# Both branch products in one loop, x added to w_out by identity products, and w_down's first weights loaded during w_up

## The chip, the cores and the metric

One core of a Trainium2 chip runs the whole kernel. Its engines are TensorE (PE, matrix products; PEld is its loading of weights), VectorE (DVE), ScalarE (ACT), GpSimd (POOL) and SyncE (SP, which issues most DMAs). The metric is the device time of one run in microseconds (us). Before the change three runs took 1689.25, 1694.08 and 1695.91 us; the median is 1694.08.

## The reference

One step of a decoder layer. The 1024 prompt positions and 8 samples of 4 positions together are T = 1056 columns; all data are float32. The part that the change touches:

```python
    mix = (jax.nn.sigmoid(gate_a) * (attn_out @ w_branch_attn)      # 256 -> 1024
           + jax.nn.sigmoid(gate_s) * (ssm_out @ w_branch_ssm))     # 512 -> 1024
    x = x + mix @ w_out                                             # 1024 -> 1024

    up = rmsnorm(x, norm2_g) @ w_up                                 # 1024 -> 2 * 2816
    a, val = up[..., :D_FF], up[..., D_FF:]
    a_ext = jnp.concatenate([conv_buf.astype(a.dtype), a], axis=1)
    a_conv = conv_b
    for i in range(CONV_W):
        a_conv = a_conv + conv_w[i] * a_ext[:, i:i + s]
    conv_state = a_ext[:, s:]
    x = x + (jax.nn.silu(a_conv) * val) @ w_down                    # 2816 -> 1024
```

Ahead of it stand a norm, the combined projection `w_in`, dilated attention over prompt and cache, and a state-space branch that ends in a gated unit (GLU); behind it stands a last norm.

## The kernel before

**Layout.** An activation is held transposed: channels on the 128 partitions, the 1056 columns side by side, so 1024 channels are eight tiles (KD = 8). The columns are ordered in four residues of C = 264 (256 prompt positions and 8 sample ones each). A float32 product is made of three products of halves: every operand is split into a rounded part (`hi`, a cast on ACT) and the rest (`lo`, a subtraction on DVE), and PE adds lo·hi, hi·lo and hi·hi. `load_w` (lines 148 to 159) does that for weights: a DMA by SP into `wraw`, the cast into `whi` (L157), the subtraction into `wlo` (L158). `gemm_k` (L165 to L178) makes the products of one 128-row output tile in three PSUM banks of 352 columns each (CH = 352, NCH = 3).

**Order.** Up to line 1218 PE's order is written by hand. After it a scheduler orders each engine's queue by its own estimates; a tile that takes the place of a former one (a pool of few buffers, or a pool that is closed and opened again at the same address) brings waits with it. SP, ACT and POOL issue DMAs in the order of their queues, and a DMA that waits holds all that stand behind it in its queue.

**Stages around the change.** (1) The attention of the samples over the cache: `cache(g, b, 1)` loads value rows by POOL's queue into a pool of four buffers, 24 loads, and PE multiplies them into one PSUM tile `pD` (L1227, L1230); then a few short steps (L1233 to L1244) put the result into `attnF`. (2) The SSM branch (L1269 to L1279): for each of eight output tiles, 36 products of w_branch_ssm, the gate loaded from `sgd` in DRAM, sigmoid on ACT, three gate multiplications on DVE, and the tile written to `msd` in DRAM. (3) x is loaded again, transposed on PE (L1281 to L1299) and written to `xtd` in DRAM. (4) The attention branch (L1324 to L1337): 18 products per output tile, gate loads from `sgd`, loads from `msd`, sigmoid, multiplication on DVE, addition on POOL, split into `mh` and `ml`. (5) w_out (L1366 to L1387): per output tile 72 products; DVE adds the tile loaded from `xtd` and writes `y`, which also goes to DRAM (`yd2`). (6) w_up (`up(f)`, 22 times), with the operands in a form in which seven block products stand for eight; the hidden tile `gt` goes to DRAM (`hd`) by POOL's queue. (7) At the end of w_up 22 transposes of conv state, then w_down (L1561 to L1602): `hidden(q)` loads hidden tiles from `hd` and splits them, and `load_w` brings weight groups of four (24 products each) into a pool `w2` whose memory is free only when w_up's tiles are.

Of the kernel before, what the change touches and what calls it, by code (L numbers as in the profile page):

```python
# [9 lines left out]
F32 = mybir.dt.float32  # L10
# [89 lines left out]
def body(tc, I, O):  # L100
# [12 lines left out]
    with root:  # L113
# [1133 lines left out]
        msd = dr.tile([D, T], F32, name="msd")  # L1247
        s5_ = root.enter_context(ExitStack())
        gl = pool("gl", 1, stack=s5_)
# [31 lines left out]
        xraw, xcol = ([t[:, j] for t in x_pairs(n, F32) for j in range(2)] for n in ("xh", "xl"))  # L1281
        xsr = go.tile([P, T], F32, name="go")[:32, :D]
        nc.sync.dma_start(xsr, I['x_sample'].rearrange("b t d -> (b t) d"))
        for s in range(S4):
            for h in range(2):
                nc.sync.dma_start(xraw[2 * s + h][:, :D], xpv[h][:, s])
        pt = pa.tile([P, 512], F32, name="pa")
        for k in range(KD):
            tr(pt[:, k * 32:(k + 1) * 32], xsr[:, k * P:(k + 1) * P])
        for k in range(KD):  # L1290
            V_.tensor_copy(sc(xcol[k])[:, :, 256:], pt[:, k * 32:(k + 1) * 32].rearrange("p (b s) -> p s b", s=S4))
        for s in range(S4):
            for k2 in range(0, KD, 2):
                pt = pa.tile([P, 512], F32, name="pa")
                for k in range(2):
                    for h in range(2):
# [340 lines left out]
```

## Time and profile before

| what | value |
|---|---|
| median of three runs | 1694.08 us |
| profiled run, its own time | 1695.59 us |
| span of the profiled run | 1693.8 us |
| PE busy | 1576.6 us, 93% |
| DVE busy | 1020.9 us, 60% |
| granted TensorE clock, mean | 0.967 |

The profile is one execution. Its span runs from the first to the last instruction, and 1.8 us of that run's time lie outside. PE is the busiest engine, but its share is a mean: the stages named above are read one by one, by tables over windows of time. A busy PE at a granted clock of 0.5 does half the work. In rows of products a `pg<-yh,wlo` names the output tile and the two operands, buffer numbers left out.

### The profile page before, as it was taken

What the parts mean: (1) busy time and instruction counts of PE and PEld (TensorE: products, weight loads), DVE (VectorE), ACT (ScalarE), POOL (GpSimd) and SP (SyncE); (2) the same over time, 40 slices, a digit from 0 to 9 for tenths busy, and PEclk for the clock granted to TensorE, in tenths of its full rate; (3) what the DMA queues carried; (4) which work ended last, traced back from release to release, by engine and by line L of the source; (5) the groups of instructions that cost most, each with busy time, mean ns of one, the idle gap of its engine ahead of it and who ended that gap; (6) DMA issues with size and microseconds to landing.
All of it is one profiled execution on the core that took longest, in us unless ns stands there. A gap on an engine that the chain in (4) does not pass through costs nothing. (4 is left out here: it accounts for less than half of the span.)

```text
span 1693.8 us, 28884 instructions
## 1 busy us (share of the span) xinstructions
PE 1576.6 (93%) x11523; PEld 1501.7 (89%) x11523; DVE 1020.9 (60%) x1655; ACT 625.1 (37%) x1135; POOL 462.7 (27%) x479
## 2 busy tenths in 40 slices
PE   5999888999999988997799999999999986999997
PEld 5899877998888878876699999999999986999997
DVE  6545989233343534322755988888888874566453
ACT  5211221144344432323544433333333334555444
POOL 0669364012122322310612022222222220121211
PEclk9899989999999999998899999999999997999998
DMA  8263322355336444676833222222222238788662
GB/s 229 64 174 112 106 60 64 99 136 134 97 100 155 132 114 167 219 232 227 260 127 115 63 76 83 82 76 77 88 78 76 76 92 284 246 264 261 196 200 96
DMA packets 272656, 234.50 MB, mean 138 GB/s; under 512 B 33269, under 2 KB 252895, under 8 KB 272522
## 3 DMA queue, kind: packets, MB, share of 16 engines
q1 hardware_dynamic: 255458, 198.65, 38.9%
q0 software_dynamic: 6496, 23.43, 3.8%
q10 hardware_dynamic: 10568, 10.58, 1.9%
q8 instruction: 90, 1.47, 0.4%
q14 instruction: 44, 0.36, 0.1%
HBM read 184.12 MB, written 50.46 MB: 138 GB/s over the span
## 5 line engine op out<-in xcount | busy, mean ns | idle before, releaser
L158 DVE TENSOR_TENSOR wlo<-wraw,whi 128x1024 fp32r<-128x1024 f32 (+1 forms) x148 | 185.4, 1255 | 155.8 <-ACT whi L157 154.6
L176 PE MATMUL pg<-xh,wlo 128*128 128x352 f32 x816 | 215.0, 345 | 1.8 <-ACT pt__5401 L872 0.5
L176 PE MATMUL pg<-xh,whi 128*128 128x352 f32 x816 | 199.9, 326 | 0.0
L176 PE MATMUL pg<-xl,whi 128*128 128x352 f32 x816 | 199.6, 326 | 0.0
L157 ACT CAST whi<-wraw 128x1024 fp32r<-128x1024 f32 (+1 forms) x148 | 147.7, 1002 | 137.8 <-PE pd L1577 89.2
L176 PEld LDWEIGHTS pg<-xh,wlo 128*128 128x128 f32 x816 | 143.7, 192 | 13.2 <-issue 5.6
L176 PEld LDWEIGHTS pg<-xl,whi 128*128 128x128 f32 x816 | 145.1, 192 | 0.3
L176 PEld LDWEIGHTS pg<-xh,whi 128*128 128x128 f32 x816 | 144.9, 190 | 0.0
L964 POOL TENSOR_TENSOR qb<-kt,qb 128x512 f32<-128x512 f32 x48 | 65.9, 1385 | 245.4 <-DMA qb<-qd 163.0
L1581 POOL COPY sy<-y 128x8 f32<-128x8 f32 x32 | 31.5, 983 | 226.0 <-DVE y L1580 225.4
L187 ACT CAST sh<-S 128x512 fp32r<-128x512 f32 x88 | 52.2, 619 | 77.1 <-DVE S L1452 52.0
L1484 POOL TENSOR_TENSOR cv<-cv,rb 128x1056 f32<-128x1056 f32 x22 | 54.2, 2464 | 72.9 <-ACT cv L1483 72.9
L1009 ACT COPY pTs<-pT 128x256 f32<-128x256 f32 (+1 forms) x48 | 22.6, 470 | 124.0 <-PE pT L145 122.1
L188 DVE TENSOR_TENSOR sl<-S,sh 128x512 fp32r<-128x512 f32 x88 | 60.6, 693 | 0.0
L176 PE MATMUL pg<-yh,wlo 128*128 128x352 f32 x144 | 48.8, 350 | 7.6 <-ACT go L473 4.9
L1480 ACT ACTIVATE cv<-ext,cw 128x1056 f32<-128x1056 f32 x22 | 28.0, 1271 | 72.8 <-POOL ext L1476 72.6
L176 PE MATMUL pg<-mh,wlo 128*128 128x352 f32 x192 | 47.5, 329 | 6.1 <-DVE wlo L158 6.1
L1467 DVE TENSOR_TENSOR ext<-ext,rb 128x528 f32<-128x528 f32 x22 | 48.5, 2207 | 0.7
L176 PE MATMUL pg<-ml,whi 128*128 128x352 f32 x192 | 47.3, 328 | 0.0
L176 PE MATMUL pg<-mh,whi 128*128 128x352 f32 x192 | 46.8, 325 | 0.0
L176 PE MATMUL pg<-yl,whi 128*128 128x352 f32 x144 | 46.5, 333 | 0.0
L176 PE MATMUL pg<-yh,whi 128*128 128x352 f32 x144 | 46.4, 335 | 0.0
(1046 smaller groups left out, 4941.2 us busy)
## 6 DMA issues: line engine op xcount, KB each, us to landing
wraw<-in_w_down_dram SPq DMA_DIRECT2D x80, 512.0 KB
wraw<-in_w_up_dram SPq DMA_DIRECT2D x44, 512.0 KB
wraw<-in_w_in_dram SPq DMA_DIRECT2D x38, 512.0 KB
qb<-qd SPq DMA_DIRECT2D x48, 256.0 KB
hd<-gt POOLq DMA_DIRECT2D x22, 528.0 KB, 3.0
wraw<-hd SPq DMA_DIRECT2D x44, 264.0 KB
sgd<-go SPq DMA_DIRECT2D x16, 528.0 KB
kt<-in_cache_kv_w_dram SPq DMA_DIRECT2D x32, 256.0 KB
```

The source lines that it names most:

```text
L157: A_.copy(hi, raw)
L158: E2.tensor_tensor(lo, raw, hi.bitcast(F32), OP.subtract)
L176: PE.matmul(ps[c][:, :CH], wt[:, k0 + k, m0:m0 + P], xt[:, c * CH:(c + 1) * CH], start=k == 0 and j == 0, stop=k == n - 1 and j == 2)
L187: A_.copy(hi, src)
L188: V_.tensor_tensor(lo, src, hi.bitcast(F32), OP.subtract)
L964: G_.tensor_tensor(qb, kv_, qb, OP.mult)
L1009: A_.copy(pTs[:, :2 * n * P], pT[:, :2 * n * P])
L1467: V_.tensor_tensor(e[:, 2:4], e[:, 2:4], h2(rb2[:, H1]), OP.mult)
L1480: A_.activation(cv, ef[:, 0:T], AF.Identity, bias=cw[:, 3, f:f + 1], scale=cw[:, 0, f:f + 1])
L1484: G_.tensor_tensor(cv, cv, rb2, OP.mult)
L1581: G_.tensor_copy(sy[:, m + x].rearrange("p (b s) -> p b s", s=S4)[:, :, q], y[:, m + x, 256:])
```

## The change

Three edits. First, SSM and attention branch become one loop: per output tile both gates are loaded, both products made, multiplied, added on POOL and split; nothing goes through `msd`. The loop uses eight PSUM banks, which are opened only when the PSUM tiles of stage (1) are closed; weights of both branches and of w_out share the pool `wo` of two buffers. Second, x is not transposed and stored ahead. `x_rows` loads rows of x as they lie in DRAM into tiles that later hold w_up's operands, and `add_x` multiplies them by a 128-column identity inside the PSUM accumulation of w_out; DVE then only copies PSUM out. The identity products are plain float32, not split. Third, the last two hidden tiles are split straight from `gt`, the first hidden loads and two weight groups of w_down are issued while w_up ends, through the pool of w_up's weights.

The core of the diff (left out are changes of names and the place of a few pools):

```diff
-        for m in range(KD):
-            if m % 2 == 0:
-                w = load_w(I['w_branch_ssm'][0][:, m * P:(m + 2) * P], 4, mw=2 * P)
-            ps = gbanks()
-            gemm(ps, w, list(zip(sh, sl)), m0=m % 2 * P)
-            t = go.tile([P, T], F32, name="go")
-            nc.sync.dma_start(t, sgd[1, m * P:(m + 1) * P])
-            A_.activation(t, t, AF.Sigmoid)
-            for c in range(NCH):
-                V_.tensor_tensor(t[:, cs(c)], ps[c][:, :CH], t[:, cs(c)], OP.mult)
-            nc.scalar.dma_start(msd[m * P:(m + 1) * P], t)
...
-            for k2 in range(0, KD, 2):
-                pt = pa.tile([P, 512], F32, name="pa")
-                for k in range(2):
-                    for h in range(2):
-                        tr(pt[:, (2 * k + h) * P:(2 * k + h + 1) * P], xraw[2 * s + h][:, (k2 + k) * P:(k2 + k + 1) * P])
-                for k in range(2):
-                    A_.copy(xcol[k2 + k][:, s * C:s * C + 256], pt[:, 256 * k:256 * k + 256])
-        xtd = dr.tile([D, T], F32, name="xtd")
-        for k in range(KD):
-            nc.sync.dma_start(xtd[k * P:(k + 1) * P], xcol[k])
...
         psum(8)
         rbp = pool("rbp", 1)
         wb = pool("wo", 2)
-        ck = pool("ck", 12, stack=s6a, side="right")
+        s6 = root.enter_context(ExitStack())
+        mp = pool("mp", 1, stack=s6)
+        mh = [mp.tile([P, T], F32R, name=f"mh{k}") for k in range(KD)]
+        ml = [mp.tile([P, T], F32R, name=f"ml{k}") for k in range(KD)]
+        ck = pool("ck", 4, stack=gst, side="right")
+        wa = None
         for m in range(KD):
+            if m % 2 == 0:
+                w = load_w(I['w_branch_ssm'][0][:, m * P:(m + 2) * P], 4, mw=2 * P, pw=wb)
             if m % 4 == 0:
-                w = load_w(I['w_branch_attn'][0][:, m * P:(m + 4) * P], 2, mw=4 * P, pw=wb)
-            ps = gbanks()
-            gemm(ps, w, list(zip(ah, al)), m0=m % 4 * P)
-            for c in range(NCH):
-                t = ck.tile([P, CH], F32, name="ck")
-                nc.sync.dma_start(t, sgd[0, m * P:(m + 1) * P, cs(c)])
+                wa = load_w(I['w_branch_attn'][0][:, m * P:(m + 4) * P], 2, mw=4 * P, pw=wb)
+            gs, ga = (ck.tile([P, T], F32, name=f"g{x}") for x in "sa")
+            for t, x in ((gs, 1), (ga, 0)):
+                nc.sync.dma_start(t, sgd[x, m * P:(m + 1) * P])
                 A_.activation(t, t, AF.Sigmoid)
-                t2 = ck.tile([P, CH], F32, name="ck2")
-                nc.scalar.dma_start(t2, msd[m * P:(m + 1) * P, cs(c)])
-                V_.tensor_tensor(t, ps[c][:, :CH], t, OP.mult)
-                G_.tensor_tensor(t, t, t2, OP.add)
-                split(mh[m][:, cs(c)], ml[m][:, cs(c)], t)
-        s6a.close()
+            for t, wt, acts, m0 in ((gs, w, zip(sh, sl), m % 2), (ga, wa, zip(ah, al), m % 4)):
+                ps = gbanks()
+                gemm(ps, wt, list(acts), m0=m0 * P)
+                for c in range(NCH):
+                    V_.tensor_tensor(t[:, cs(c)], ps[c][:, :CH], t[:, cs(c)], OP.mult)
+            G_.tensor_tensor(ga, ga, gs, OP.add)
+            split(mh[m], ml[m], ga)
+        gst.close()
...
+        def x_rows(j):
+            pk = max(1, j // 2 + 1)
+            n0 = 4 * (j % 2)
+            out = []
+            for i, m in enumerate((j, j + NK)):
+                halves = []
+                for h in range(2):
+                    n = n0 + 2 * i + h
+                    t = xa.tile([P, HALF], F32, name=f"x{pk}{n // 2}{'hl'[n % 2]}")[:, :512].rearrange("p (s f) -> p s f", s=S4)
+                    nc.sync.dma_start(t, xpv[h][:, :, m * P:(m + 1) * P])
+                    halves.append(t)
+                n = 8 + i
+                t = xa.tile([P, HALF], F32, name=f"x{pk}{n // 2}{'hl'[n % 2]}" if j % 2 == 0 else f"x{pk}5{'hl'[i]}")[:32, :P]
+                nc.sync.dma_start(t, I['x_sample'].rearrange("b t d -> (b t) d")[:, m * P:(m + 1) * P])
+                out.append((halves, t))
+            return out
+        def add_x(ps, halves, xs):
+            for s in range(S4):
+                for h in range(2):
+                    a = s * C + h * P
+                    while a < s * C + (h + 1) * P:
+                        c = a // CH
+                        e = min(s * C + (h + 1) * P, (c + 1) * CH)
+                        i0 = a - s * C - h * P
+                        PE.matmul(ps[c][:, a - c * CH:e - c * CH], halves[h][:, s], ident[:, i0:i0 + e - a],
+                                  start=False, stop=False)
+                        a = e
+                a = s * C + 256
+                c = a // CH
+                PE.matmul(ps[c][:, a - c * CH:a - c * CH + NB], xs, ident[:32, s:32:S4], start=False, stop=False)
+        def steps(ps, w, ks):
+            for k in ks:
+                for j in range(3):
+                    wt, xt = ((1, 0), (0, 1), (0, 0))[j]
+                    for c in range(NCH):
+                        PE.matmul(ps[c][:, :CH], w[wt][:, k], (mh, ml)[xt][k][:, cs(c)],
+                                  start=k == 0 and j == 0, stop=k == KD - 1 and j == 2)
+        rows = {0: x_rows(0)}
         for j in range(NK):
-            ys = []
-            for m in (j, j + NK):
-                w = load_w(I['w_out'][0][:, m * P:(m + 1) * P], KD, pw=wb)
-                ps = gbanks()
-                gemm(ps, w, list(zip(mh, ml)))
+            ys, early = [], {}
+            if j < NK - 1:
+                rows[j + 1] = x_rows(j + 1)
+            else:
+                for i in range(2):
+                    m = j + i * NK
+                    w, ps = load_w(I['w_out'][0][:, m * P:(m + 1) * P], KD, pw=wb), gbanks()
+                    steps(ps, w, [0])
+                    add_x(ps, *rows[j][i])
+                    early[m] = w, ps
+            for i, m in enumerate((j, j + NK)):
+                if m in early:
+                    w, ps = early[m]
+                    steps(ps, w, range(1, KD))
+                else:
+                    w, ps = load_w(I['w_out'][0][:, m * P:(m + 1) * P], KD, pw=wb), gbanks()
+                    steps(ps, w, range(KD - 1))
+                    add_x(ps, *rows[j][i])
+                    steps(ps, w, [KD - 1])
                 y = yt_.tile([P, T], F32, name="yt", bufs=3)
-                nc.sync.dma_start(y, xtd[m * P:(m + 1) * P])
                 for c in range(NCH):
-                    V_.tensor_tensor(y[:, cs(c)], ps[c][:, :CH], y[:, cs(c)], OP.add)
+                    V_.tensor_copy(y[:, cs(c)], ps[c][:, :CH])
                 nc.sync.dma_start(yd2[m * P:(m + 1) * P], y)
...
+        first = []
         for f in range(NF):
-            up(f)
+            gt = up(f)
+            if f >= NF - 2:
+                first.append(gt)
+        places = [(k, o) for o in (0, 4, 1, 3, 5, 2, 6) for k in range(NK)]
+        NH = NF // 2
+        def place(q, j):
+            k, o = places[q % 2 * NH + j]
+            pl = xa if k < NK - 1 else xb
+            return [pl.tile([P, HALF], F32R, name=f"x{k}{o}{x}") for x in "hl"]
+        def hidden_pair(q, j):
+            hi, lo = place(q, j)
+            r = wb.tile([P, KD, P], F32, name="wraw").rearrange("p k m -> p (k m)")[:, :HALF]
+            nc.sync.dma_start(h2(r), hd[2 * j * P:(2 * j + 2) * P, q * C:(q + 1) * C].rearrange("(f p) c -> p f c", p=P))
+            split(hi, lo, r)
+            return [(hi[:, x * C:(x + 1) * C], lo[:, x * C:(x + 1) * C]) for x in range(2)]
+        def hidden(q, js=range(NH)):
+            return [p for j in js for p in hidden_pair(q, j)]
+        def w_group(m, k0, **kw):
+            n = min(4, NF - k0)
+            return load_w(I['w_down'][0][k0 * P:(k0 + n) * P, m * P:(m + 2) * P], n, mw=2 * P, **kw)
+        hs_ = hidden(0, range(4))
+        ahead = [w_group(0, 0, pw=wb)]
+        hs_ += hidden(0, range(4, 8))
+        ahead.append(w_group(0, 4, pw=wb))
+        hs_ += hidden(0, range(8, NH - 1))
+        hi, lo = place(0, NH - 1)
+        for x in range(2):
+            p_ = hi[:, x * C:(x + 1) * C], lo[:, x * C:(x + 1) * C]
+            split(*p_, first[x][:, :C])
+            hs_.append(p_)
...
-                    w = load_w(I['w_down'][0][k0 * P:(k0 + n) * P, m * P:(m + 2) * P], n, mw=2 * P, pw=w2,
-                               bufs=({"bufs": 4}, {}))
+                    w = ahead.pop(0) if ahead else w_group(m, k0, pw=w2, bufs=({"bufs": 4}, {}))
```

PE's order where the cache values are multiplied. `pD<-cache` are the value products of stage (1), `pg<-yh` and `pg<-yl` those of the SSM branch, `ident,dD` the transpose that ends stage (1). Before:

```order
L176 MATMUL pg<-yh_7200,wlo 128x352 x2
L176 MATMUL pg<-yl_7204,whi 128x352 x2
L176 MATMUL pg<-yh_7200,whi 128x352 x2
L1227 MATMUL pD<-cache,Pm 32x256 x4
L176 MATMUL pg<-yh_7201,whi 128x352
L176 MATMUL pg<-yh_7201,wlo 128x352
L176 MATMUL pg<-yl_7205,whi 128x352
L176 MATMUL pg<-yh_7201,whi 128x352
L1227 MATMUL pD<-cache,Pm 32x256 x4
```

The same place after the change:

```order
L1230 MATMUL pD<-cache,Pm 128x256
L1227 MATMUL pD<-cache,Pm 32x256 x8
L1230 MATMUL pD<-cache,Pm 128x256
L1227 MATMUL pD<-cache,Pm 32x256 x8
L145 MATMUL pa<-ident,dD 128x128
L176 MATMUL pg<-yh_7197,wlo 128x352
L176 MATMUL pg<-yl_7201,whi 128x352
L176 MATMUL pg<-yh_7197,whi 128x352
```

The value products stood between SSM products and now stand in one row, with all SSM products behind them.

PE's order in the first w_out tile, after the change; `x10h`, `x10l` and `x14h` hold rows of x here, and `mh`, `ml` are the halves of the gated sum:

```order
L1371 MATMUL pg<-mh_7244,whi 128x352 x3
L1371 MATMUL pg<-mh_7245,wlo 128x352
L1359 MATMUL pg<-ident,x10h 128x128
L1359 MATMUL pg<-ident,x10h 128x40
L1371 MATMUL pg<-mh_7245,wlo 128x352
L1359 MATMUL pg<-ident,x10l 128x128
L1364 MATMUL pg<-ident,x14h 128x8
L1359 MATMUL pg<-ident,x10h 128x88
L1359 MATMUL pg<-ident,x10l 128x128
L1364 MATMUL pg<-ident,x14h 128x8
```

Fourteen such products (ten of `ident` with prompt rows, four of eight columns with sample rows) stand in each of the eight w_out tiles, where before only the 72 products of `mh` and `ml` stood.

SP's queue where w_up's weights end (`wraw<-in_w_up_dram`) and w_down's begin. Before:

```order
L1443 DMA wraw<-in_w_up_dram 128x8x128 x42
L1509 DMA wraw<-hd 128x2x264 x11
L1563 DMA y<-yd_8219 128x8x264
L156 DMA wraw<-in_w_down_dram 128x4x256 x4
L1509 DMA wraw<-hd 128x2x264 x2
L1563 DMA y<-yd_8219 128x8x264
L156 DMA wraw<-in_w_down_dram 128x4x256
L156 DMA wraw<-in_w_down_dram 128x2x256
```

After:

```order
L1466 DMA wraw<-in_w_up_dram 128x8x128 x42
L1529 DMA wraw<-hd 128x2x264 x4
L156 DMA wraw<-in_w_down_dram 128x4x256
L1529 DMA wraw<-hd 128x2x264 x4
L156 DMA wraw<-in_w_down_dram 128x4x256
L1529 DMA wraw<-hd 128x2x264 x6
L1607 DMA y<-yd_7909 128x8x264
L156 DMA wraw<-in_w_down_dram 128x4x256 x3
L156 DMA wraw<-in_w_down_dram 128x2x256
```

Two weight groups of w_down now stand between the hidden loads; the next three stand behind six more hidden loads and the load of `y`, and their first waits for the last store of `gt` to `hd`.

## Rows read from the trace of the kernel before

**Rows 1.** the page, part 1: busy us, share of the span, instructions of each engine.

```profile
PE 1576.6 (93%) x11523; PEld 1501.7 (89%) x11523; DVE 1020.9 (60%) x1655; ACT 625.1 (37%) x1135; POOL 462.7 (27%) x479
```

**Rows 2.** windows: bounds in us, length, busy us (instructions), granted clock, DMA share, GB/s.

```profile
core 0: us, PE busy (x) PEld busy (x) DVE busy (x) ACT busy (x) POOL busy (x), PEclk, DMA share, GB/s
711.00:756.00 45.00, 41.84 (x285) 33.26 (x284) 10.92 (x19) 8.48 (x8) 12.67 (x16) 0.96 0.80 261
756.00:774.00 18.00, 17.90 (x112) 17.58 (x111) 8.27 (x15) 4.95 (x8) 0.00 (x0) 1.00 0.43 151
774.00:790.00 16.00, 11.86 (x70) 9.12 (x71) 3.79 (x11) 10.42 (x31) 0.00 (x0) 0.80 0.54 162
790.00:806.00 16.00, 8.30 (x52) 8.01 (x50) 0.00 (x0) 1.24 (x4) 0.00 (x0) 0.82 0.83 317
806.00:834.00 28.00, 18.92 (x97) 16.63 (x97) 23.83 (x41) 19.91 (x44) 23.63 (x21) 0.87 0.88 291
834.00:840.00 6.00, 6.00 (x26) 6.00 (x27) 5.83 (x9) 2.48 (x6) 3.97 (x4) 0.66 0.71 187
840.00:929.00 89.00, 88.64 (x552) 88.34 (x550) 47.93 (x66) 36.10 (x44) 15.14 (x7) 1.00 0.38 127
1388.00:1414.00 26.00, 4.30 (x24) 2.92 (x25) 7.89 (x10) 8.84 (x12) 3.90 (x5) 0.62 0.54 178
1414.00:1430.00 16.00, 16.00 (x117) 16.00 (x117) 9.35 (x10) 7.10 (x9) 0.00 (x0) 0.86 1.03 326
1430.00:1682.00 252.00, 251.07 (x2067) 250.38 (x2066) 138.89 (x177) 123.99 (x173) 45.10 (x41) 1.00 0.69 217
```

**Rows 3.** PE groups, 692 to 840 us: busy us, mean ns, idle before it, releaser.

```profile
L176 PE MATMUL pg<-ah,wlo 128*128 128x352 f32 x48 | 17.2, 358 | 10.7 <-DVE ck L1335 10.7
...
L145 PE MATMUL pa<-ident,xh 128*128 128x128 f32 x64 | 11.9, 347 | 2.6 <-ACT xl L1299 2.2 <-DVE xl L1291 0.4
...
L176 PE MATMUL pg<-mh,wlo 128*128 128x352 f32 x9 | 3.4, 456 | 6.1 <-DVE wlo L158 6.1
```

**Rows 4.** the tile cache, 690 to 760 us: duration ns min/median/max, first and last start.

```profile
L1227 PE MATMUL pD<-cache,Pm x128: 379/379/403, 702.9 to 755.4; 128*32 128x256 f32 x128
...
L1177 POOL DMA_DIRECT2D cache<-in_cache_kv_w_dram x14: 748/748/794, 703.2 to 743.8; - x14
L1175 POOL DMA_DIRECT2D cache<-in_cache_kv_w_dram x6: 549/549/567, 704.7 to 739.8; - x6
...
DMA to landing us min/median/max: 3.7/5.9/9.3
```

**Rows 5.** timeline of PE: start us, us, what; then weight loads of L1405 (ns).

```profile
258.75 1.05 PE L750 MATMUL pa<-U,em 128*128 128x264 f32 x4
...
934.64 1.99 PE L1405 MATMUL pe<-ones,rb 128*128 128x1 f32 x18
...
L1405 PEld LDWEIGHTS pe<-ones,rb x18: 106/192/192, 934.5 to 936.4; 128*128 128x128 f32 x16, 128*32 128x32 f32 x2
```

**Rows 6.** DVE, ACT and POOL groups, 692 to 850 us, columns as in rows 3.

```profile
L1278 DVE TENSOR_TENSOR go<-pg,go 128x352 f32<-128x352 f32 x24 | 11.7, 520 | 38.1 <-ACT go L1276 22.8 <-PE pg L176 8.1 <-issue 7.1
...
L188 DVE TENSOR_TENSOR al<-attnF,ah 128x1056 fp32r<-128x1056 f32 x2 | 2.5, 1254 | 1.5 <-PE pg L176 1.5
...
L1276 ACT ACTIVATE go<-go 128x1056 f32<-128x1056 f32 x8 | 8.7, 1085 | 39.6 <-DMA go<-sgd 39.6
...
L1264 POOL TENSOR_TENSOR sf<-sf,go 128x1056 f32<-128x1056 f32 x3 | 7.4, 2461 | 7.8 <-ACT go L1263 7.8
```

**Rows 7.** the chain that ended last, 1370 to 1420 us: start, us, what.

```profile
1404.69 6.51 DMA wraw<-in_w_down_dram
1411.22 1.05 ACT whi L157
1412.30 1.24 DVE wlo L158
...
1413.58 6.51 PE pd L1577 x34
```

More of the change, by code (lines that the diff above doesn't have):

```diff
@@ L1244, in body @@
                         pt[r, :P].rearrange("p (t h b) -> p t h b", t=4, h=4)[:, :, 2 * pr + h])
-        msd = dr.tile([D, T], F32, name="msd")
-        s5_ = root.enter_context(ExitStack())
-        gl = pool("gl", 1, stack=s5_)
+        gst = root.enter_context(ExitStack())
+        gl = pool("gl", 1, stack=gst, side="right")
         yh = [gl.tile([P, T], F32R, name=f"yh{k}") for k in range(4)]
@@ L1268, in body @@
             split(sh[k], sl[k], sf[k])
[L1269 to L1313 removed]
+        s4.close()
+        ap_ = pool("ap", 1, stack=gst, side="right")
         ah = [ap_.tile([P, T], F32R, name=f"ah{k}") for k in range(2)]
@@ L1342, in body @@
+            G_.tensor_tensor(ga, ga, gs, OP.add)
+            split(mh[m], ml[m], ga)
+        gst.close()
         NK = KD // 2
         rb1 = rbp.tile([P, T], F32, name="rb1")
-        cso = rbp.tile([P, NF, 18], F32, name="cso")
-        xa = pool("xa", 1)
+        xas = root.enter_context(ExitStack())
+        xa = pool("xa", 1, stack=xas, side="right")
         XO = [None] * NK
         s6y = root.enter_context(ExitStack())
-        yt_ = pool("yt", 1, stack=s6y)
+        yt_ = pool("yt", 1, stack=s6y, side="right")
@@ L1364, in operands @@
                 XO[k][o] = (hi, lo)
-        kept = []
-        for j in range(NK):
-            ys = []
-            for m in (j, j + NK):
-                w = load_w(I['w_out'][0][:, m * P:(m + 1) * P], KD, pw=wb)
-                ps = gbanks()
-                gemm(ps, w, list(zip(mh, ml)))
+        def x_rows(j):
[14 more added lines that the diff above has]
+            return out
@@ L1388, in body @@
         s6.close()
-        xb = pool("xb", 1, side="right")
+        cso_ = pool("cso", 1)
+        cso = cso_.tile([P, NF, 18], F32, name="cso")
+        xb = pool("xb", 1)
         operands(NK - 1, xb, *ys)
@@ L1486, in up @@
             nc.gpsimd.dma_start(hd[f * P:(f + 1) * P], gt)
+            return gt
+        first = []
         for f in range(NF):
-            up(f)
+            gt = up(f)
[28 more added lines that the diff above has]
+            hs_.append(p_)
         s7.close()
@@ L1497, in body @@
         pt_ = pool("pt", 4, PSUM, stack=s9)
-        places = [(k, o) for o in (0, 4, 1, 3, 5, 2, 6) for k in range(NK)]
-        NH = NF // 2
-        def hidden(q):
-            out = []
-            for j in range(NH):
-                k, o = places[q % 2 * NH + j]
-                pl = xa if k < NK - 1 else xb
-                hi, lo = (pl.tile([P, HALF], F32R, name=f"x{k}{o}{x}") for x in "hl")
-                r = wb.tile([P, KD, P], F32, name="wraw").rearrange("p k m -> p (k m)")[:, :HALF]
-                nc.sync.dma_start(h2(r), hd[2 * j * P:(2 * j + 2) * P, q * C:(q + 1) * C].rearrange("(f p) c -> p f c", p=P))
-                split(hi, lo, r)
-                out += [(hi[:, x * C:(x + 1) * C], lo[:, x * C:(x + 1) * C]) for x in range(2)]
-            return out
         gf = rb1[:, :D]
@@ L1559, in body @@
         G_.memset(fr, 1.0)
-        hs_ = hidden(0)
         for q in range(S4):
```

8 lines of the change are left out of this document (removed).

## The prediction

> **What bounds the kernel now.** I read the page's shares of the engines first: PE is busy 93% of the span, no other engine over 60% [rows 1]. So the time is what PE waits for and what its clock loses. Next the windows over the stages that the change touches [rows 2]. From 711 to 774 us, where SSM products and value products alternate, PE is busy nearly throughout at a granted clock near 1.00. From 774 to 840 us it is not: it works 11.86 of 16 us (transposes of x), 8.30 of 16, 18.92 of 28 and 6.00 of 6, with granted clocks between 0.66 and 0.87, so part of it at the lower level of 1.2 GHz. From 840 to 929 us w_out fills PE at full clock. From 1388 to 1414 us, between w_up and w_down, PE is busy 4.30 of 26 us, and then 16 us run at 0.86, until from 1430 us on w_down runs full. The groups by line say what ends the waits [rows 3]: 10.7 us ahead of the attention products until DVE's gate multiplication, and 6.1 us ahead of w_out's first product until its weights are split. The chain of waits shows the gap at w_down [rows 7]: the first w_down loads go out at 1404.69 us, land 6.51 us later, are cast and subtracted, and PE starts at 1413.58.
>
> So the change takes work from a stretch that is badly filled, puts new work into one that is full, and fills part of a gap.
>
> **Part 1: one loop for both branches.** The 64 large transposes of x go (11.9 us busy), and with them the second pass through DRAM and the attention products' wait. What stays on PE is 8 × (36 + 18) = 432 products of 352 columns. w_out's 552 records fill 88.64 us at full clock [rows 2], 0.1606 us each; 432 of them are 69.4 us.
>
> But the loop starts later. Its PSUM banks open only when the value products are done, and these lose their cover: in the order before, SSM products stand between them, afterwards nothing does. The 20 loads that POOL still issues from 703.2 us on (14 of 512 KB, 6 of 128 KB, 8.13 MB) go through four buffers [rows 4]. From below, DMA alone sets the pace: at the 317 GB/s of the window 790 to 806 us [rows 2] they take 25.6 us, and with a last landing of about 3 us the row ends at 732. From above, every round of four pays a median landing of 5.9 us, an issue of 0.75 us and about 1 us of products: 5 × 7.65 = 38 us, and with one more landing that began late, 745. In the trace before, POOL issued the last one at 743.8 us and the last value product began at 755.4, because PE came late. The first rounds are the same as before, and four loads overlap in part, so I take 737.
>
> Behind it stand steps that nothing covers: mask and reductions on DVE, a transpose, four copies, two casts and two subtractions of 1056 columns (1.25 us each on DVE [rows 6]). The SSM products of the first tile need only the PSUM banks, some 2 us, so they start at 739. The gate loads need memory that the attention tiles held until the second subtraction (about 6.6 us after the value products, an estimate from the steps of DVE and ACT), and all later gate loads queue behind the first on SP. With 4 us for the load, 1.09 us for the sigmoid and 0.52 us for a multiplication [rows 6], the first bank comes free some 12.4 us after the value products; PE needs it after 2 + 9.6 us (60 products). That is a wait near 1 us. A POOL addition of 1056 columns takes 2.46 us and a subtraction 1.25 us per output tile [rows 6], against 8.7 us of products, so neither is the bound. Weights: the pool of two buffers makes a new group wait for the product two groups before; cast and subtraction (2.3 us by the chain [rows 7]) are covered by 18 attention products (2.9 us), narrowly. After the thin row of value products I charge 2.5 us of lower clock (the windows 774 to 840 show that such rows run at 0.66 to 0.87). Together I charge 4 us, between 1 and 9. w_out starts at 739 + 69.4 + 4 = 812.4 us instead of 834: **−21.6 us**, between −29 and −9.
>
> **Part 2: x added on PE.** Each output tile gets 14 plain float32 products, and each of these is two records in the trace (L1405 makes nine products, one for each block of columns, and shows 18 records [rows 5]). The price of a record with 128 columns is not shown. L1405 multiplies a single column by 128 × 128 weights at full clock: 18 records in 1.99 us, 0.11 us each, so new float32 weights cost that much however few the columns are. L750's four records of 264 columns fill 1.05 us, 0.26 us each; scaled by columns, the 1056 columns of an output tile cost 2 × 1056 × 0.26/264 = 2.1 us. If the loading of weights (192 ns in PEld [rows 5]) were exposed in full, 28 × 0.19 = 5.4 us. Nearest are the L1405 rows, since each product here changes its weights and has at most 128 columns: 28 × 0.11 = 3.1 us per tile, **+24.6 us** for eight, between +17 and +43. This falls into the stretch where PE is full, so nothing hides it. DVE's copies of PSUM take the place of its additions and were hidden anyway.
>
> The Trainium skill (FP8 and Floating Point Precision, TensorE Precision Notes) says that true FP32 takes four passes through the array. By that rule 1056 columns × 4 at 2.4 GHz would be an estimated 1.76 us per tile, +14 us in all. L750's row is near it (1056 columns for 2.1 us), L1405's is not, since one column costs as much there as 128 would by the rule.
>
> Rows of x come as loads on SP's queue that wait for the memory of operands or gates freed late in the loop, and stand behind w_out's weight loads, whose first ones wait for splits. The first ones are needed about 11 us after w_out starts, and land at about that time: +1 us, between 0 and 5. w_out's own weights no longer wait 6.1 us [rows 3]; that is in the start time above.
>
> **Part 3: the gap ahead of w_down.** Two of six weight groups are there early, 48 products. From 1430 to 1682 us 2067 records fill 251.07 us [rows 2], 0.1215 us each, so 5.8 us of work move into the gap. The rest of the gap stays, since the next loads still wait for the last store of `gt` to `hd`: its chain (the last gate, POOL's multiplication, the store) ends where the first w_down load goes out before, 1404.69 us [rows 7]. PE then idles some 13 us still, and again starts at a lower clock. SP has two weight groups and four more hidden loads ahead of these loads, in two buffers at some 5 us each; by my count that ends at about 1403 us, just in time. **−6 us**; if more of the gap goes −12, if the queue is late +3.
>
> **Sum** against the profiled run of 1695.59 us: −21.6 + 24.6 + 1 − 6 = −2.0, so 1693.6 us, and on the median of 1694.08, which lies 1.5 us lower, **1692 us**. A difference under 0.5% (8.5 us) can't be told from none in this kernel, so the forecast is "the same".
>
> **Rivals.** (a) Faster, by columns: the identity products cost what their columns cost, as L750 shows, because PE loads the next weights beside the running product (PEld is busy 88.34 of 89 us in w_out [rows 2], which speaks against free room, but products of `mh` overlap it there too). +17 instead of +24.6, with value loads at the pace of DMA alone (−5 more): 1679 us. The four-pass rule named above (the Trainium skill, FP8 and Floating Point Precision, TensorE Precision Notes) speaks for a price by columns and would put it 3 us lower. (b) Slower, weights exposed: each of the 28 records of a tile pays the 192 ns that PEld shows in L1405 [rows 5], +43 instead of +24.6: 1710 us. For it: switching between split and plain products has no row. Against it: L1405's own records are 0.11 us apart. It decides for "slower" from 0.158 us a record on. (c) Slower, value products uncovered: each round pays its whole landing, the row ends at 745 and the loop's first gate behind it, +8, and rows of x 5 us late: 1704 us. For it: landings up to 9.3 us [rows 4]; against it: DMA has less beside it. (d) Handover without gain: the first loads for the rest go out later than 1404.69 us because SP's queue is longer, and what PE did early it waits for later: 1698 us.
>
> **Chances.** Forecast (within 8.5 us of before, about 1685 to 1701) 0.42; (d) 0.10, also "the same"; (a) and its parts 0.27; (b) 0.12; (c) 0.09. So faster 0.27, same 0.52, slower 0.21. The range 1677 to 1707 us takes in (a) and (c) with some of the gap's −12, and leaves out about one in ten on each side: most of (b), and (a) with more of the gap.
>
> **What would show it.** In the profile after: the last value product starts near 737 us (732 to 745), with PE waiting for cache loads between; the first w_out product near 812; identity records 0.11 us apart (0.075 on average in rival a, 0.19 in b); w_up's first products near 933 instead of 929; PE works some 6 us between w_up and w_down and waits until about 1416. Wrong would be: value products that end after 750, a loop in which PE waits for gates or weights in each tile, or a w_down that starts its third weight group earlier than 16 us after the last w_up product.

## The result, and the profile after the change

The kernel after the change took 1712.16 us (median of 4 runs, 1711.07 to 1715.15), the kernel before 1694.99 in the same comparison: a ratio of 1.0109, interval 1.0081 to 1.0138. It is about 1% slower. The forecast was 1692 us, "the same", with 1707 as the upper end: the time lies above the range, and the kernel got slower where the sum had it 2 us faster.

The profiled run took 1711.07 us with a span of 1709.3, against 1695.59 and 1693.8 before: +15.5 us. Part 1 of the page after (answers to [rows 1]):

```profile
PE 1595.8 (93%) x11675; PEld 1519.6 (89%) x11675; DVE 1016.6 (59%) x1632; ACT 617.4 (36%) x1072; POOL 455.5 (27%) x463
```

PE is busy 19.2 us longer in 152 records more (224 of identity products come, 72 of transposes go), and its share is unchanged: the shares say nothing about where the time went. The windows do (after, columns as in [rows 2]):

```profile
711.00:737.00 26.00, 15.35 (x88) 4.02 (x88) 2.44 (x4) 0.00 (x0) 7.16 (x11) 0.50 0.70 236
737.00:756.00 19.00, 18.73 (x109) 18.71 (x109) 6.50 (x11) 11.55 (x15) 2.48 (x1) 0.92 0.67 257
756.00:812.00 56.00, 52.43 (x325) 51.91 (x324) 33.16 (x51) 20.64 (x20) 14.80 (x6) 1.00 0.34 106
812.00:840.00 28.00, 28.00 (x179) 27.21 (x177) 9.18 (x10) 6.08 (x6) 2.47 (x1) 1.00 0.85 230
840.00:939.00 99.00, 99.00 (x626) 95.56 (x625) 39.03 (x57) 32.49 (x39) 16.12 (x6) 1.00 0.19 61
939.00:960.00 21.00, 12.41 (x80) 11.82 (x79) 18.14 (x34) 11.40 (x17) 2.72 (x4) 0.76 0.24 76
1405.00:1431.00 26.00, 8.68 (x70) 7.79 (x70) 12.48 (x13) 10.04 (x15) 3.76 (x5) 0.78 0.67 216
1431.00:1447.00 16.00, 12.08 (x81) 12.08 (x82) 7.43 (x9) 7.95 (x11) 0.00 (x0) 0.72 0.99 315
1447.00:1698.00 251.00, 249.88 (x2058) 249.20 (x2056) 136.32 (x174) 122.12 (x171) 45.54 (x41) 1.00 0.68 213
```

The reader is to see four things. The value products (711 to 737) now run thinly at a granted clock of 0.50, the level of 1.2 GHz. The loop of both branches (737 to 812) is well filled. w_out (812 to 939) is filled without a gap at full clock, and lasts longer than before. And two stretches are thinner than the forecast had them: the start of w_up (in its first 21 us, 941 to 962, PE is busy 13.57 us at 0.76; in the kernel before, 929 to 950, it was 17.70 at 0.92) and the start of w_down.

The tile `cache` after, 690 to 760 us (answers to [rows 4]):

```profile
L1227 PE MATMUL pD<-cache,Pm x128: 379/632/637, 696.3 to 734.9; 128*32 128x256 f32 x128
...
  PE pD L1227: 14.3, 12
...
DMA to landing us min/median/max: 2.7/5.5/8.1
```

The second line stands under "who waited for it": PE waited 14.3 us in 12 waits for cache loads, and the last product of the row began at 734.9 us.

The stages, from the starts of PE's products in the traces (us; "w_out" is the time from its first to its last product, "rest" from w_up's last product to w_down's last one):

| kernel | last value product | w_out starts | w_out | w_up | rest |
|---|---|---|---|---|---|
| before | 755.43 | 833.85 | 94.47 | 458.31 | 293.51 |
| after | 734.88 | 812.21 | 126.75 | 464.02 | 291.95 |
| after less before | | -21.64 | +32.28 | +5.71 | -1.56 |

With +0.55 between w_out and w_up (0.93 to 1.48 us) and +0.14 behind w_down's last product the differences sum to +15.48, all of what the profiled runs differ by. So the experiments ask three things: why x in PSUM costs 32 us and not 25, what holds w_up for 5.7 us, and why the handover gives 1.6 us and not 6.

### The profile page after: what moved, and what is told of

It is laid out like the page before. It is cut to its first block, busy times and chain, and to the rows that moved or that the text cites. A ratio compares the mean times of both kernels' runs of the same rounds, so it can differ in the third digit from the quotient of the medians.

```text
span 1709.3 us, 28903 instructions
## 1 busy us (share of the span) xinstructions
PE 1595.8 (93%) x11675; PEld 1519.6 (89%) x11675; DVE 1016.6 (59%) x1632; ACT 617.4 (36%) x1072; POOL 455.5 (27%) x463
## 4 chain that ended last, share of the span: by engine, by line
PE 51%; DMA 4%; DVE 2%; issue 1%; ACT 1%; SPq 0%; POOL 0%; ACTq 0%; DVEq 0%; POOLq 0%
PE pu L1454 25%; PE pd L1620 13%; PE pg L1371 6%; PE pg L176 4%; DMA wraw<-hd 2%; PE pg L1359 1%; DMA cache<-in_cache_kv_w_dram 1%; DMA ga<-sgd 1%; PE pg L1364 1%; DMA wraw<-in_w_down_dram 0%; PE pt L145 0%; DVE wlo L158 0%; PE pD L1227 0%; DVE gs L1300 0%; ACT whi L157 0%
## 5 line engine op out<-in xcount | busy, mean ns | idle before, releaser
L158 DVE TENSOR_TENSOR wlo<-wraw,whi 128x1024 fp32r<-128x1024 f32 (+1 forms) x148 | 183.7, 1244 | 147.0 <-ACT whi L157 144.9
L964 POOL TENSOR_TENSOR qb<-kt,qb 128x512 f32<-128x512 f32 x48 | 65.1, 1370 | 247.7 <-DMA qb<-qd 134.9
L1397 DVE COPY yt<-pg 128x352 f32<-128x352 f32 x24 | 11.1, 519 | 61.4 <-PE pg L1371 61.4
L176 PE MATMUL pg<-yh,wlo 128*128 128x352 f32 x144 | 42.3, 333 | 5.7 <-DVE wlo L158 3.6
L1500 POOL COPY ext<-cbf 128x16 f32<-128x16 f32 x22 | 15.7, 714 | 115.6 <-DVE cv L1504 115.6
L1404 POOL TENSOR_TENSOR rb<-rb,tt 128x1056 f32<-128x1056 f32 x7 | 18.6, 2652 | 104.0 <-ACT tt L1403 85.4
L1499 POOL COPY ext<-ext 128x510 f32<-128x510 f32 x22 | 13.3, 604 | 123.7 <-DVE ext L1496 123.7
L473 ACT COPY go<-pg 128x352 f32<-128x352 f32 x48 | 21.2, 452 | 65.7 <-issue 43.5
```

The lines of the kernel that those rows point to most:

```text
L158: E2.tensor_tensor(lo, raw, hi.bitcast(F32), OP.subtract)
L176: PE.matmul(ps[c][:, :CH], wt[:, k0 + k, m0:m0 + P], xt[:, c * CH:(c + 1) * CH], start=k == 0 and j == 0, stop=k == n - 1 and j == 2)
L964: G_.tensor_tensor(qb, kv_, qb, OP.mult)
```

## The experiments

Each starts from the kernel after the change; line numbers in the diffs are left out, and each ratio is to the kernel before on the same chip.

**x left out.** `e1_no_x`: the sum in w_out without x, and no loads of its rows.

```diff
-                    add_x(ps, *rows[j][i])
```

> This kernel leaves x out of the sum in w_out (no identity products, no loads of rows of x); all else is the changed kernel. Theory A (the identity products cost what the trace of the changed kernel shows, 4.12 us per output tile, and PE has nothing else to do there): 8 x 4.12 = 33 us less, about 1679 us; w_out lasts 94 to 95 us instead of 127. Rival B (the products take the place of waits that come back, such as weights or splits of the gated sum that are late): less than 20 us less, about 1693 us or more, with PE waiting inside w_out.

Measured 1676.73 us, ratio 0.9899 [0.9858, 0.994]; w_out 93.0 us. So everything that x costs in w_out is 126.7 - 93.0 = 33.7 us. (The kernel before took 94.5 us for the same products without x; its first 6 us there ran at a granted clock of 0.66 [rows 2].) The 1% against the kernel before is not the gain of the other parts, since this kernel leaves out all work on x.

**Sample rows together.** `e2_rows32`: the same 14 products per tile, the four with sample rows behind the ten with prompt rows instead of between them.

```diff
                         a = e
+            for s in range(S4):
                 a = s * C + 256
```

> The four products with sample rows (32 rows by 8 columns) stand in one row at the end of each tile's identity products instead of between the prompt ones. Theory A (the price lies in the change between products of 128 and of 32 weight rows: 0.205 us into one and 0.181 us out of it, against 0.11 and 0.13 within): the identity products of a tile fall from 4.12 to about 3.3 us, 6 to 7 us in all, about 1705 us. Rival B (a product of 32 rows costs 0.52 us wherever it stands): no change, 1712 us.

Measured 1706.67 us, 1.0083 [1.0054, 1.0112]; w_out 120.2 us. PE's timeline of one tile's identity products in the kernel after (start us, us, what; two records for each product):

```profile
838.24 0.38 PE L1359 MATMUL pg<-ident,x11h 128*128 128x128 f32 x2
838.46 0.39 PE L1359 MATMUL pg<-ident,x11l 128*128 128x128 f32 x2
838.77 0.38 PE L1364 MATMUL pg<-ident,x14l 32*128 32x8 f32 x2
839.09 0.64 PE L1359 MATMUL pg<-ident,x11h 128*128 128x88 f32 x4
839.55 0.47 PE L1359 MATMUL pg<-ident,x11l 128*128 128x128 f32 x2
839.95 0.38 PE L1364 MATMUL pg<-ident,x14l 32*128 32x8 f32 x2
...
842.04 0.38 PE L1364 MATMUL pg<-ident,x14l 32*128 32x8 f32 x2
842.36 0.76 PE L1371 MATMUL pg<-mh,wlo 128*128 128x352 f32 x3
```

And the end of such a tile with the samples together:

```profile
839.70 0.43 PE L1359 MATMUL pg<-ident,x11h 128*128 128x128 f32 x2
839.97 0.39 PE L1359 MATMUL pg<-ident,x11l 128*128 128x128 f32 x2
840.28 1.05 PE L1365 MATMUL pg<-ident,x14l 32*128 32x8 f32 x8
841.26 0.75 PE L1372 MATMUL pg<-mh,wlo 128*128 128x352 f32 x3
```

Read the distances of the starts. Two records of 128 rows and 128 columns: 838.46 - 838.24 = 0.22 us, 0.11 each, as forecast. From `x11l` to the 32-row `x14l` and on to the next 128-row record: 838.46 to 838.77 and 838.77 to 839.09, 0.31 and 0.32, each about 0.1 longer. Split into single records, these are 0.11 between two of 128 rows, 0.205 from 128 to 32 rows, 0.133 between the two of 32 and 0.181 back; single starts around the short products (88, 48 and 40 columns) scatter more, and do so with the samples together too, so it is the sums that tell. One tile's 28 records take 4.12 us with four such changes there and back; with one change, 3.31 us (837.96 to 841.26), and the eight 32-row records in a row are again about 0.11 apart.

**The rows filled to 128.** `e15_rows128`: the order of the kernel after, but the sample rows stand in a tile of 128 rows, 96 of them zero, and no record has 32 rows.

```diff
-...[:32, :P]
+...[:, :P]
+                G_.memset(t, 0.0)
-                PE.matmul(ps[c][:, ...], xs, ident[:32, s:32:S4], start=False, stop=False)
+                PE.matmul(ps[c][:, ...], xs, ident[:, s:32:S4], start=False, stop=False)
```

> The sample rows of x lie in tiles of 128 rows whose other rows are zero, so that every identity product has 128 weight rows; the order is that of the changed kernel, with sample products between prompt ones. Theory A (it is the change between 128 and 32 weight rows that costs, 0.27 us for each pair of changes): the identity products of a tile take 28 x 0.11 = 3.1 us instead of 4.12, 8 us in all, about 1704 us. Rival B (it is the jump to other columns, banks or the small size that costs): 4.1 us a tile again and 1712 us.

Measured 1704.55 us, 1.0057 [1.0032, 1.0082]; w_out 117.9 us. This settles it: the same products in the same order without a change of row count cost 117.9 - 93.0 = 24.9 us (one tile's 28 records take 3.04), and the prediction's 28 × 0.11 × 8 is 24.6. The remaining 126.7 - 117.9 = 8.8 us are the changes between 128- and 32-row weights, 32 pairs of them, about 0.27 us a pair. `e2_rows32` agrees: its eight pairs make 120.2 - 117.9 = 2.3 us, 0.28 a pair.

**The sums of weights first.** `e5_sides`: the pools of w_up's temporaries and of the weights' sums `S`, `sh`, `sl` exchange sides, so that `S` no longer lies on the memory of the tiles `yt` and `tt` that make w_up's operands (in the kernel after, `sr` is opened on the right side, where the pool of `yt` and `tt` was closed just before).

```diff
-        ff = pool("ff", 1, stack=s7)
-        sr = pool("sr", 1, stack=s7, side="right")
+        ff = pool("ff", 1, stack=s7, side="right")
+        sr = pool("sr", 1, stack=s7)
```

> The pool of w_up's weight sums and the pool of its work tiles change sides of SBUF, so that the weight sums no longer lie where w_out's y tiles lay. Theory A (the first sums stand behind all splits of the last operands on DVE because of that memory, and PE waits 6.9 us for them): the wait falls to 1 to 3 us, as before the change, 4 to 6 us less, about 1707 us. Rival B (DVE has simply too much to do there, and the operands' splits become late instead): within 1.5 us of 1712 us.

Measured 1707.07 us, 1.0075 [1.0048, 1.0102]; w_up 459.2 us instead of 464.0, and 458.3 before; in the other kernels with the sides of the kernel after it took 463.0 to 464.4. DVE's timeline at the start of w_up, in the kernel after:

```profile
940.29 0.70 DVE L188 TENSOR_TENSOR x30l<-yt,x30h 128x528 fp32r<-128x528 f32 x1
...
949.05 0.69 DVE L188 TENSOR_TENSOR x36l<-tt,x36h 128x528 fp32r<-128x528 f32 x1
949.66 0.15 DVE L250 TENSOR_SCALAR n<-n 128x9 f32<-128x9 f32 x1
949.74 0.67 DVE L1474 TENSOR_TENSOR S<-wraw 128x512 f32<-128x512 f32 x1
```

With the sides exchanged:

```profile
941.89 1.39 DVE L1397 COPY yt<-pg 128x352 f32<-128x352 f32 x3 [7.55 <-PE pg L1371]
943.19 0.68 DVE L1474 TENSOR_TENSOR S<-wraw 128x512 f32<-128x512 f32 x1
943.79 0.69 DVE L1476 TENSOR_TENSOR S<-wraw 128x512 f32<-128x512 f32 x1
```

And in the kernel before:

```profile
929.11 0.68 DVE L1451 TENSOR_TENSOR S<-wraw 128x512 f32<-128x512 f32 x1
```

In the first `S` stands behind the last operand split, 9.3 us after w_up's first product (940.4); in the second it is the first thing after the copies of PSUM, 0.1 us ahead of w_up's first product (943.3), as in the kernel before (929.2). PE's group that needs `sl` says what that costs (last number: idle time and releaser); the kernel after, 940 to 1406 us:

```profile
L1454 PE MATMUL pu<-x04h,sl 128*128 128x264 f32 x44 | 12.9, 294 | 6.9 <-DVE sl L188 6.9
```

with the sides exchanged, 943 to 1404 us:

```profile
L1454 PE MATMUL pu<-x04h,sl 128*128 128x264 f32 x44 | 13.1, 297 | 2.3 <-DVE sl L188 2.3
```

and the kernel before, 929 to 1390 us:

```profile
L1431 PE MATMUL pu<-x04h,sl 128*128 128x264 f32 x44 | 12.9, 293 | 1.0 <-DVE sl L188 1.0
```

6.9 against 2.3: the 4.6 us are nearly all of what w_up got shorter by (4.9).

**The handover.** After w_up's last product at 1404.5 us the two early groups run from 1407.6 to about 1415.5, and PE then waits for the third, until 1434.9. SP's queue in the kernel after (start us, us, what; one row may hold several issues with waits between):

```profile
1404.10 0.37 SPq L156 DMA_DIRECT2D wraw<-in_w_down_dram  x1
1406.94 15.91 SPq L1529 DMA_DIRECT2D wraw<-hd  x6
1422.97 0.42 SPq L1607 DMA_DIRECT2D y<-yd  x1
1423.56 3.67 SPq L156 DMA_DIRECT2D wraw<-in_w_down_dram  x4
```

and the end of the chain there (answers to [rows 7]):

```profile
1424.08 7.61 DMA wraw<-in_w_down_dram
...
1432.57 1.05 ACT whi L157
1433.61 0.02 issue
1433.64 1.24 DVE wlo L158
1434.87 0.04 issue
1434.92 5.17 PE pd L1620 x22
```

The last store of `gt` to `hd`, for which the third load waits by its memory, is issued by POOL at 1418.41:

```profile
1418.41 0.59 POOL L1509 DMA_DIRECT2D hd<-gt  x1 [2.04 <-DVE gt L1508]
```

It lands 4.3 us later, at 1422.7, which is 18.3 us after w_up's last product; in the kernel before it landed 16.0 us after it. SP stands in hidden loads until 1422.8, so both come free at the same time. Two possible holders: memory and queue. Three kernels take them away, first one by one, then together.

`e7_memory`: `w2` lies on tiles that are done earlier, and `y` is loaded behind the first weights. Its core:

```diff
+            gt = ff.tile([P, T], F32, name="gt", bufs=2)
+            cv = ff.tile([P, T], F32, name="cv")
             r1, u2, u3, u4 = (h2(ff.tile([P, HALF], F32, name=n)) for n in ("r1", "u2", "u3", "u4"))
-            gt = ff.tile([P, T], F32, name="gt", bufs=2)
...
-            cv = ff.tile([P, T], F32, name="cv")
```

> Only the memory wait ahead of w_down's later weight groups is taken away: the tiles gt and cv change places with smaller tiles in w_up's work pool, so that the new weight pool no longer lies on gt and cv, and the load of y goes out behind the weights. The four hidden loads of the next residue still stand ahead of them on SP's queue. Theory A (two causes, each enough by itself: the memory of the last hidden tile and the queue of hidden loads): no gain beyond 2 us, about 1710 to 1712 us, first later load still near 1422 us. Rival B (memory alone holds the loads back): they go out near 1408 us, 10 us or more less, 1702 us or below.

`e10_queue`: the hidden loads of the second residue stay behind what the program writes ahead of them.

```diff
-            nc.sync.dma_start(h2(r), hd[...])
+            d = nc.sync.dma_start(h2(r), hd[...])
+            if q == 1:
+                tc.keep_in_program_order(d)
```

> Only the queue is changed: the hidden loads of the next residue are kept behind the weight groups on SP's queue; the weight pool still lies on gt and cv and waits for the last store. Theory A (two causes, each enough by itself): no gain beyond 2 us, about 1710 to 1712 us, since the store lands near 1421.5 us. Rival B (the queue alone holds them back): 8 us or more less, 1704 us or below.

`e9_both`: both edits.

> Both together: weight pool off the last hidden tiles, and hidden loads of the next residue behind the weight groups; three split groups as in the changed kernel. Theory A: the later groups' loads go out between 1407 and 1412 us, the third group starts near 1418 us instead of 1435, 12 to 16 us less, about 1697 us, without the waits at each group that two split groups brought. Rival B (what is gained in the gap is lost behind it, to DMA that has to bring the hidden tiles of the next residue): 5 us less at most, 1707 us.

Measured: memory alone 1716.00 us, 1.0133 [1.0106, 1.0161]; queue alone 1712.38, 1.0101 [1.0073, 1.0129]; both 1704.56, 1.0055 [1.0034, 1.0076]. Each alone brings nothing, both bring about half a per cent: each cause suffices to hold the load. Counted from w_up's last product of each kernel, the first of the four loads goes out after 19.1 us in the kernel after, 20.5 with memory alone, 23.4 with the queue alone and 14.8 with both. (The profiled run with memory alone was 7 us above its median.) SP's queue with memory alone:

```profile
1414.72 17.90 SPq L1529 DMA_DIRECT2D wraw<-hd  x6
1432.73 2.82 SPq L156 DMA_DIRECT2D wraw<-in_w_down_dram  x4
```

with the queue alone:

```profile
1418.70 0.36 SPq L1609 DMA_DIRECT2D y<-yd  x1
1427.46 2.02 SPq L156 DMA_DIRECT2D wraw<-in_w_down_dram  x4
```

with both:

```profile
1408.37 4.17 SPq L1529 DMA_DIRECT2D wraw<-hd  x2
1420.60 5.87 SPq L156 DMA_DIRECT2D wraw<-in_w_down_dram  x4
```

With memory alone the loads stand behind six hidden loads. With the queue alone they wait for the store of `gt`, which lands at 1427.0; what SP's queue waited for there, 1402 to 1430 us:

```profile
SPq L156 <- DMA hd<-gt: 8.0, 1, 8.0
```

With both, PE's wait for the split weights (L158) falls from 19.5 to 10.1 us and the rest from 291.9 to 284.5 us. That is less than expected, since a third holder shows, in the same view of that kernel:

```profile
SPq L156 <- DMA out_dram<-wlo: 12.3, 4, 8.0
```

The trace puts these waits to the store of the conv state, which is staged in a `wlo` tile of the weights' pool. Taking that away was not tried; `c3_combined` below still has it.

`e6_w2`: two buffers for `w2` instead of three, which puts them on other memory.

```diff
-        w2 = pool("w2", 3, stack=s9, side="right")
+        w2 = pool("w2", 2, stack=s9, side="right")
```

> The pool of w_down's weights holds two split groups instead of three, so that it fits into the memory of the weight sums and no longer waits for the last hidden tile and its store. Theory A (the gap behind the first two weight groups is there because the next loads go out only at 1423.6 us, behind that store and four more hidden loads): the loads go out near 1405 us, the third group starts at about 1415 us instead of 1435, 12 to 18 us less, about 1697 us. Rival B (two split groups are too few, or DMA can't bring both weights and hidden tiles at that time): less than 6 us less, since w_down waits later by what it gained.

Measured 1724.69 us, 1.0176 [1.0126, 1.0225]. The third group does start at 1417.8, and no long gap is left there, but PE's waits from 1400 us on are

```profile
PE pd L1620 <- DVE wlo L158: 20.2, 24, 2.5
```

24 short ones instead of two: what was one wait is spread over w_down, and the rest is 304.6 us. Moving a wait forward by shrinking a pool did not pay.

`e4_old_handover`: the handover of the kernel before, the other two parts of the change as they are.

```diff
-        hs_ = hidden(0, range(4))
-        ahead = [w_group(0, 0, pw=wb)]
-        hs_ += hidden(0, range(4, 8))
-        ahead.append(w_group(0, 4, pw=wb))
...
+        ahead = []
+        hs_ = hidden(0)
```

> Part 3 alone undone in the changed kernel: hidden tiles and w_down's weights are loaded as before the change. From the last w_up product to the last w_down product took 293.5 us before and 291.9 us after. Theory A (the two early weight groups gain nothing, since what stands behind them waits as much longer): within 2.5 us of 1712 us. Rival B (they gain the 6 us that I predicted and the rest of the stage lost it for another reason): 5 to 8 us slower, about 1718 us.

Measured 1713.52 us, 1.0115 [1.0084, 1.0146], against 1.0109 [1.0081, 1.0138] of the full change: part 3 gains nothing that can be measured here, though each interval is about 5 us wide to either side. (The profiled run of this kernel was 8 us above its median, so its stages are not set beside the others'.) The stages of other kernels point the same way: `e1_no_x`, `e2_rows32`, `e15_rows128` and `e13_x_early` below have part 3 as it is, and their rest took 293.1 to 294.1 us, against 293.5 in the one profile of the kernel before. The 1.6 us of the kernel after lie within what such executions differ by. `e4_old_handover` also shows that part 3 itself holds up the last store of `gt`: without it the store lands 15.5 us after w_up's last product (16.0 in the kernel before), with it 18.3 to 20.5 us after (the kernel after and the four named). DVE's queue in the kernel after shows what stands between the steps of the last hidden tile (`cv`, `gt`):

```profile
1409.51 1.23 DVE L158 TENSOR_TENSOR wlo<-wraw,whi 128x1024 fp32r<-128x1024 f32 x1 [0.75 <-ACT whi L157]
1410.65 1.31 DVE L1505 SCALAR_TENSOR_TENSOR cv<-ext,cw,cv 128x1056 f32<-128x1056 f32 x1
```

That `wlo` is the split of an early weight group, which the kernel before had not yet loaded there.

**x elsewhere.** `e13_x_early`: x is transposed again, but between the value products, where PE waits for cache loads; w_out adds it on DVE as before.

```diff
+            for _ in range(2):
+                k2, s = turns.pop(0)
+                x_turn(k2, s)
...
-                    V_.tensor_copy(y[:, cs(c)], ps[c][:, :CH])
+                    V_.tensor_tensor(y[:, cs(c)], ps[c][:, :CH], y[:, cs(c)], OP.add)
```

> Part 2 undone in another place: x is transposed on PE as in the kernel before and added by DVE in w_out, but its 72 transposes stand between the GLU and value products, where PE waits for cache loads (14.3 us in the changed kernel). Loop and handover are those of the changed kernel. Theory A (the identity products cost 33 us in a stretch that is full, the transposes are nearly free in one that waits): 26 to 33 us less, about 1682 us; the loop starts at most 6 us later than at 737 us. Rival B (loads and stores of x, 13 MB more, hold up the cache loads, which set the end of the value products): the loop starts 10 to 20 us later, and the time is 1690 to 1700 us.

Measured 1681.43 us, 0.9927 [0.9905, 0.9949]; the last value product at 736.5 us, w_out 93.0 from 814.4 us on. The transposes were nearly free (window of that kernel, columns as above):

```profile
711.00:737.00 26.00, 18.44 (x140) 12.13 (x139) 6.26 (x5) 13.00 (x26) 10.99 (x11) 0.88 0.93 317
```

52 records more than after in the same 26 us, at a clock of 0.88 instead of 0.50; the last value product begins 1.6 us later and w_out starts 2.1 us later. Other kernels differ by more in that (742.5 us in `e7_memory`, which has no transposes there), so the price of the transposes is not resolved, only that it is small beside 33.7 us.

**All together.** `c3_combined`: `e13`'s x, the sides of `e5` (with those of `w2` and `fb` exchanged too), `y` behind the first weights and the pinned loads of `e10`.

```diff
-        w2 = pool("w2", 3, stack=s9, side="right")
-        fb = pool("fb", 2, stack=s9)
+        w2 = pool("w2", 3, stack=s9)
+        fb = pool("fb", 2, stack=s9, side="right")
```

> What the runs so far point to, together: the loop of the change; x transposed early, between the GLU and value products, and added by DVE; the weight sums of w_up away from the y tiles; w_down's weights off the last hidden tiles and ahead of the next residue's hidden loads. If the gains add up, 1681 us less 5 (weight sums) and less 7.5 (handover): about 1669 us. If the handover's gain was one with the longer kernel alone, 1676 us.

Measured 1669.37 us, 0.984 [0.9812, 0.9869]: 1.6% faster than the kernel before. Against the kernel after, its w_out is 33.7 us shorter (93.0), its w_up 5.6 (458.4), its rest 10.3 (281.7), and w_out starts 8.0 later, at 820.2: -41.6, as the profiled runs differ.

## Why the prediction was wrong, by its own steps

**The start of the loop: right.** Value products until 737 us forecast (732 to 745), 735 measured; w_out at 812.4 forecast, 812.2 measured; -21.6 in both. In the loop PE waited 3.6 us for two weight splits and for no gate; the forecast had charged 4 us for such things and the low clock together. That it came out to 0.2 us is partly luck: the value products ended 2.1 us early, the stretch from there to w_out was 1.9 us longer than forecast, and in other kernels the value products ended up to 8 us later.

**x in PSUM: the price of a record right, a term missing.** Forecast +24.6 for identity products and +1 for rows of x; measured +32.3. `e15_rows128` confirms the 0.11 us per record [rows 5] to 0.3 us in the sum (24.9 us), as a mean over records of 8 to 128 columns. The step that failed is 28 × 0.11 as one price: the 28 records are of two kinds, 128-row and 32-row weights, laid in turns, and the change between them, which the sum put at nothing, took 8.8 us. The hint was in [rows 5] itself, whose L1405 group holds 16 loads of 128 rows and 2 of 32: the 1.99 us were divided by 18 as if all were one kind. Rival (a), a price by columns (+17 against 24.9), falls; so does (b), exposed weight loads: 4.12/28 = 0.147 us a record lies under its 0.19 and under the 0.158 from which it was to decide. The kernel was slower without (b), from two more terms. Rows of x cost nothing: PE is busy 28.00 of 28 and 99.00 of 99 us in w_out. The Trainium skill's four passes for true FP32 (FP8 and Floating Point Precision, TensorE Precision Notes) made an estimated 1.76 us a tile; the traces disagree for products this small, with 3.04 us at best (`e15_rows128`).

**w_up: not seen.** No step of the prediction says anything of w_up but its start (forecast 933, measured 940.4). The change opens pools in another order and on other sides, so the sums of weights lie on memory that the last w_out tiles hold, and DVE does them last: +5.7 us, of which `e5_sides` takes back 4.9.

**The handover: half right.** Forecast: 5.8 us of products move into the gap, and the third group starts about 25 us after w_up ends, as the first did before (26.0). The two groups do run there, from 1407.6 to 1415.5; but the third starts 30.5 us after w_up ends. Two steps failed. One is "SP has two weight groups and four more hidden loads ahead of these loads": it counted w_down's first residue only. Four of the six hidden loads in SP's row from 1406.94 belong to the next residue, wait for the splits that free their two buffers, and hold the queue until 1422.8. The other is that the store of `gt` would end as before: counted from w_up's end it landed 2.3 us later than in the kernel before, and `e4_old_handover` shows that part 3 is what delays it. This is rival (d), in which the moved work is waited for later; it was put at 0.10 and at 1698 us. `e9_both` shows that memory and queue must both go; without that no gain of the part can be measured (`e4_old_handover`).

In sum: +6.7 from x, +6.3 in w_up and just ahead of it, +4.4 at the handover and +0.1 at the end make the 17.5 us between the forecast of 1693.6 for the profiled run and its 1711.1.

What stays open: the last value product fell between 733.2 and 742.5 us in kernels whose code is alike up to there or nearly so (742.5 in `e7_memory` and in `c3_combined`), and with it everything behind it; what sets this was not tried.

## What to carry to other kernels

Work moved onto the engine that bounds the kernel is paid in full, so price each kind of it: the small products here cost 0.11 us per record, and each change of their row count and back 0.27 us more. Put work that must be done into a stretch where that engine waits for DMA instead (33.7 us less in w_out, against a start of w_out 2.1 us later). When pools are opened in another order, read which later tile now lies on whose memory, and which loads stand ahead in its queue: a wait with two sufficient causes does not move until both are gone.

## What the runs showed of the hardware

- A plain float32 product is two records. With weights of 128 rows in all of them, 28 records of 8 to 128 columns took 3.04 us, 0.11 us each on average, and 224 of them 24.9 us (`e15_rows128`).
- Changing from 128-row to 32-row weights and back costs about 0.27 us a pair (8.8 us for 32 pairs). Grouping them takes most of that away (3.31 us instead of 4.12 a tile), filling the 32 rows up with zero rows all of it (3.04 us a tile, w_out 117.9 instead of 126.7 us).
- Transposes between products that wait for DMA raised the granted clock of that stretch from 0.50 to 0.88, and its last product began 1.6 us later (`e13_x_early`).
